# Loads of w by slot, four heads in banks of their own, and the first quarter of w from SyncE as float32

## The chip, the cores and the metric

One core of one Trainium2 chip. The metric is device time in microseconds (us), the median of several runs.

## The reference

```python
B, S, D = (16, 2048, 1024)          # x: B x S x D, w: D x D, decay: D, all float32
xw = x @ w
out[:, 0, :] = xw[:, 0, :]
for t in range(1, S):
    out[:, t, :] = decay * out[:, t - 1, :] + xw[:, t, :]
```

So: a matrix product, then a decayed running sum along S.

## The kernel before

x is cut into 64 chunks of 512 time steps. A chunk is loaded by GpSimd with a cast to bfloat16 (`xb`), turned on VectorE (`xw`), copied to `xt` by ScalarE or VectorE, and multiplied by w on TensorE: two chunks are one group, and each of the 8 column blocks n ("heads") of a group is one tile of 16 matmuls of 512 columns, accumulated in PSUM. A tile is then scanned along time on VectorE. Six of eight tiles are scanned in pairs of steps, for which ScalarE and GpSimd do the other half of the arithmetic; the factor of such a scan is decay squared (`dec2`). The order of all this is a fixed list of deeds per tile, the agenda. w lies in SBUF as `wsb[:, k, ...]` with k = 2m + e: m is a slot of 64 rows in each quarter of 256 rows, e tells even rows from odd ones; q is the quarter of the 128 partitions.

Its parts that change (cut):

```python
dec2 = psp.tile([128, 512], FP32, name="dec2")          # squares of decay, a PSUM bank
...
def load_w(queue, h, e, m0=0, m1=M):                    # 4 loads of 32 partitions
    for q in range(NQ):
        pin(queue.dma_start(
            out=stage[h, e, m0][quad(q)].rearrange("p (m d) -> p m d", m=m1 - m0),
            in_=_ap(w, [[2 * D, P], [2 * P * D, m1 - m0], [1, CH]],
                    (q * CQ + m0 * 2 * P + e) * D + h * CH)))
...
for _ in range(34):                                     # warm-up
    pin(nc.tensor.matmul(out=spare, lhsT=idle[:, 0:128], rhs=idle, start=True, stop=True))
load_w(nc.sync, 0, 0, 0, M // 2)                        # float32; all other loads of w: GpSimd, cast
...
# agenda: M = half a chunk of x, U = a group of loads of w, W/w = copy of w on VectorE/ScalarE,
#         E/F/G = turn and copies of half a chunk, P/S/C/B = a tile's pairing, scan, completion, output
-99: "M0 M1 U0 U1 M2 M3 U2 U3 L L L W0 w1 E0 F0 G0 w3 W2 E1 F1 G1 W4 w5 ...",
...
if step == 0:                                           # three heads with two banks each, one with one
    heads = [ring(psp, "ps", 3, [128, T]) for _ in range(3)]
    firsts = [ps[:, 0:TL] for ps in heads] + [spare]
```

## Time and profile before

| | before |
|---|---|
| time, median of 4 runs beside the changed kernel | 915.33 us (915.03 to 915.55) |
| span of the profiled run | 912.5 us |
| TensorE, VectorE, ScalarE, GpSimd busy | 891, 826, 686, 664 us |
| first real matmul; end of the last | 11.2; 901.6 us |
| half clock of TensorE | only up to 6.6 us, and after its work has ended |

The rest of the reading is in the prediction. Views in order of time show start, duration, line, operation, out<-in, what ended the idle time before. First, VectorE in order of time (start, duration, line, operation, out<-in, what ended the idle time before): the turns of the four half chunks. Three begin as soon as the half chunk has landed; the second landed at 11.2 and waited for another deed.

```profile
8.60 1.25 DVE L115 STREAM_TRANSPOSE xw<-xb 128x1024 f32<-128x1024 f32 x1 [1.55 <-DMA xb<-in_x_dram]
12.87 1.24 DVE L115 STREAM_TRANSPOSE xw<-xb 128x1024 f32<-128x1024 f32 x1
18.61 1.25 DVE L115 STREAM_TRANSPOSE xw<-xb 128x1024 f32<-128x1024 f32 x1 [2.38 <-DMA xb<-in_x_dram]
21.33 1.25 DVE L115 STREAM_TRANSPOSE xw<-xb 128x1024 f32<-128x1024 f32 x1 [0.17 <-DMA xb<-in_x_dram]
```

Second, the time from issue to landing of all twenty loads of w:

```profile
DMA to landing us min/median/max: 2.7/4.4/5.7
```

### The profile page before, as it was taken

Reading aid. Unit: us, or ns where it says so; the run is one execution under the profiler, and the core shown is the slowest. Engines: PE = TensorE matmul, PEld = TensorE weight load, DVE = VectorE, ACT = ScalarE, POOL = GpSimd, SP = SyncE. Lnnn points to the kernel's source line nnn. Section 1 sums busy time; section 2 is a strip of 40 time slices with the busy share of each in tenths; the row PEclk is TensorE's granted clock in tenths of the full one; section 3 lists DMA queues with packets and bytes.
Section 4 is the critical chain, followed back from the end, with each engine's and each line's share of the span. In section 5 each row is a group of like instructions: output and inputs, shape, how many; then the busy total and the mean of one; then the engine's idle time right before and its main releaser. Section 6 shows DMA issues by size and latency. Waiting matters only on the chain.

```text
span 912.5 us, 11926 instructions
## 1 busy us (share of the span) xinstructions
PE 891.3 (98%) x4088; PEld 408.5 (45%) x4170; DVE 826.0 (91%) x613; ACT 685.8 (75%) x950; POOL 664.4 (73%) x764
## 2 busy tenths in 40 slices
PE   8899999999999999999999999999999999999995
PEld 4444444444444444444444444444444444444442
DVE  4999999999999999999999999999999999999986
ACT  3778887877877777778778778778778778777753
POOL 8688878777777777777677777777787776776552
PEclk9999999999999999999999999999999999999998
DMA  9999999999999999999999999999999999999668
GB/s 170 166 220 215 215 230 235 256 250 255 247 237 255 247 237 224 230 233 231 223 235 227 224 231 229 230 226 231 227 224 230 231 230 224 232 229 207 151 151 219
DMA packets 406253, 204.49 MB, mean 224 GB/s; under 512 B 12976, under 2 KB 405936, under 8 KB 406192
## 3 DMA queue, kind: packets, MB, share of 16 engines
q1 hardware_dynamic: 268848, 134.76, 59.5%
q0 software_dynamic: 137344, 68.96, 56.8%
q8 instruction: 32, 0.52, 0.2%
q14 instruction: 29, 0.24, 0.1%
HBM read 138.42 MB, written 134.22 MB: 299 GB/s over the span
## 4 chain that ended last, share of the span: by engine, by line
PE 90%; DMA 3%; POOL 2%; issue 2%; DVE 2%; ACT 1%; SPq 0%; DVEq 0%; POOLq 0%
PE ps L126 90%; DMA xb<-in_x_dram 2%; POOL xb L105 1%; DMA ot<-in_w_dram 1%; DVE so L194 1%; DVE xw L115 1%; POOL ot L245 1%; PE spare L126 0%; DMA out_dram<-ot 0%; DVE so L180 0%; POOL so L208 0%; ACT xt L123 0%; DVE ot L215 0%; POOL xs L174 0%; ACT xs L168 0%
## 5 line engine op out<-in xcount | busy, mean ns | idle before, releaser
L126 PE MATMUL ps<-xt,wsb 128*128 128x512 bf16 (+1 forms) x4011 | 874.2, 377 | 9.0 <-DVE so L194 2.6
L126 PEld LDWEIGHTS <-wsb 128*128 128x128 bf16 x4136 | 404.6, 98 | 485.7 <-issue 5.6
L174 POOL TENSOR_TENSOR xs<-h,xs 128x512 f32<-128x512 f32 (+1 forms) x193 | 245.3, 1271 | 195.5 <-ACT h L158 88.3
L168 ACT COPY xs<-ps 128x1024 f32<-128x1024 f32 (+1 forms) x193 | 191.6, 993 | 158.8 <-PE ps L126 149.3
L215 DVE STREAM_TRANSPOSE ot<-so 128x1024 f32<-128x1024 f32 (+1 forms) x264 | 302.7, 1184 | 1.9 <-POOL so L208 1.1
L208 POOL TENSOR_TENSOR so<-h,xs 128x512 f32<-128x512 f32 (+1 forms) x193 | 244.3, 1266 | 34.5 <-ACT h L158 18.1
L123 ACT COPY xt<-xw 128x2048 bf16<-128x2048 bf16 (+1 forms) x128 | 239.8, 1875 | 7.5 <-DVE xw L115 7.5
L105 POOL DMA_DIRECT2D xb<-in_x_dram x264 | 174.1, 660 | 2.0 <-POOLq L435 0.9
L158 ACT ACTIVATE h<-so,dec 128x512 f32<-128x512 f32 (+1 forms) x193 | 147.1, 763 | 36.0 <-DVE so L180 32.1
L115 DVE STREAM_TRANSPOSE xw<-xb 128x2048 f32<-128x2048 f32 (+1 forms) x66 | 146.7, 2222 | 6.1 <-DMA xb<-in_x_dram 6.1
L180 DVE TENSOR_TENSOR_SCAN so<-dec,keep,xs 128x512 f32<-128x512 f32 (+1 forms) x99 | 121.6, 1229 | 29.8 <-POOL xs L174 29.6
L180 DVE TENSOR_TENSOR_SCAN so<-dec,xs 128x512 f32<-128x512 f32 x94 | 114.8, 1222 | 31.3 <-POOL xs L174 28.2
L158 ACT ACTIVATE h<-ps,dec 128x512 f32<-128x512 f32 (+1 forms) x193 | 131.8, 683 | 0.0
L194 DVE TENSOR_TENSOR_SCAN so<-dec,ps 128x1024 f32<-128x1024 f32 x33 | 74.5, 2261 | 0.0
L194 DVE TENSOR_TENSOR_SCAN so<-dec,keep,ps 128x1024 f32<-128x1024 f32 (+1 forms) x33 | 73.4, 2225 | 0.0
L211 ACT COPY keep<-so 128x1 f32<-128x1 f32 x136 | 25.1, 187 | 0.3 <-DVE so L194 0.3
L173 ACT COPY so<-keep 128x1 f32<-128x1 f32 x99 | 19.0, 192 | 0.7 <-DVE ot L215 0.7
L171 POOL MEMSET so<- 128x1 f32 x94 | 11.0, 117 | 3.2 <-DVE ot L215 3.2
L262 PE MATMUL spare<-idle 128*128 128x512 bf16 x34 | 10.2, 473 | 1.2 <-DVE idle L259 1.2
L126 PE MATMUL spare<-xt,wsb 128*128 128x512 bf16 (+1 forms) x43 | 11.2, 359 | 0.1
L245 POOL DMA_DIRECT2D ot<-in_w_dram x16 | 9.0, 561 | 2.4 <-issue 0.7
L253 ACT COPY wsb<-ot 128x512 bf16<-128x512 bf16 x6 | 3.4, 615 | 5.7 <-DMA ot<-in_w_dram 5.7
(18 smaller groups left out, 20.3 us busy)
## 6 DMA issues: line engine op xcount, KB each, us to landing
out_dram<-ot SPq DMA_DIRECT2D x248, 512.0 KB, 10.6
xb<-in_x_dram POOLq DMA_DIRECT2D x248, 256.0 KB, 7.8
out_dram<-ot SPq DMA_DIRECT2D x12, 256.0 KB, 4.2
xb<-in_x_dram POOLq DMA_DIRECT2D x16, 128.0 KB, 5.0
ot<-in_w_dram POOLq DMA_DIRECT2D x12, 128.0 KB, 5.2
out_dram<-ot SPq DMA_DIRECT2D x8, 128.0 KB, 2.8
ot<-in_w_dram SPq DMA_DIRECT2D x4, 128.0 KB, 3.5
ot<-in_w_dram POOLq DMA_DIRECT2D x4, 64.0 KB, 4.3
```

The costliest lines, as they stand in the source:

```text
L105: pin(nc.gpsimd.dma_start(out=xb_of[c][quad(q), j0:j1], in_=_ap(x, [[D, P], [P * D, j1 - j0], [1, CQ]], (b * S + t0 + j0 * P) * D + q * CQ)))
L115: pin(nc.vector.transpose(out=dst.rearrange("p (m j i) -> p j m i", m=M, i=P)[:, j0:j1], in_=src.rearrange("p (j m c) -> p j m c", m=M, c=P)))
L123: pin(copy(out=xt_of[c][:, m0:m1, :, j0 * P:j1 * P], in_=src))
L126: pin(nc.tensor.matmul(out=ps[:, t0:t1], lhsT=wsb[:, k, n].rearrange("p q i -> p (q i)"), rhs=xt[:, k // 2, k % 2, t0:t1], start=(k == 0 a ...
L158: pin(nc.scalar.activation(out=h, in_=src, func=mybir.ActivationFunctionType.Copy, scale=dec[:, self.n:self.n + 1]))
L168: pin(nc.scalar.copy(out=self.xs, in_=self.ps))
L174: pin(nc.gpsimd.tensor_tensor(out=self.xs[:, 1:T:2], in0=g, in1=self.xs[:, 1:T:2], op=ALU.add))
L180: pin(nc.vector.tensor_tensor_scan(out=so[:, 3:T + 2:2], data0=dec2[:, n:n + 1].to_broadcast([128, T // 2]), data1=self.xs[:, 1:T:2], init ...
L194: pin(nc.vector.tensor_tensor_scan(out=so[:, t:t + size], data0=dec[:, n:n + 1].to_broadcast([128, size]), data1=ps, initial=before, op0=A ...
L208: pin(nc.gpsimd.tensor_tensor(out=so[:, 2:T + 2:2], in0=h, in1=self.xs[:, 0:T:2], op=ALU.add))
L211: pin(nc.scalar.copy(out=self.keep, in_=so[:, T + 1:T + 2]))
L215: pin(nc.vector.transpose(out=self.ot[:, :, n % R * P:(n % R + 1) * P], in_=self.so[:, 2:T + 2].rearrange("p (i t) -> p i t", t=P)))
```

## The change

The intent: w becomes usable slot by slot (one load of 128 partitions brings all that one k needs) instead of only when all four quarters are there; all four heads of the first group run through before the first scan, each with banks of its own; and GpSimd, which issues all the casting loads of both kernels, gives more of w to SyncE. To free a bank for the fourth head the squares of decay move to SBUF, and after some tiles to a spare bank. The core of the diff (cut: bookkeeping for outputs, which keeps the same order; the turns and copies of x in two pieces; the order of the first group's matmuls; and the agenda of steps 0 to 16):

```diff
-    dec2 = psp.tile([128, 512], FP32, name="dec2")
+    squares = [const.tile([128, K], FP32, name="squares")]
 ...
-    def load_w(queue, h, e, m0=0, m1=M):
-        for q in range(NQ):
-            pin(queue.dma_start(
-                out=stage[h, e, m0][quad(q)].rearrange("p (m d) -> p m d", m=m1 - m0),
-                in_=_ap(w, [[2 * D, P], [2 * P * D, m1 - m0], [1, CH]],
-                        (q * CQ + m0 * 2 * P + e) * D + h * CH)))
+    def load_w(queue, i):
+        h, e, m = i // 8, i // 4 % 2, i % 4
+        pin(queue.dma_start(
+            out=stage[h, e][:, m * CH:(m + 1) * CH],
+            in_=_ap(w, [[CQ * D, NQ], [2 * D, P], [1, CH]], (m * 2 * P + e) * D + h * CH)))
 ...
-    for _ in range(34):
+    pin(nc.scalar.copy(out=idle[:, 0:1], in_=idle[:, 1:2]))
+    for _ in range(27):
 ...
-    load_w(nc.sync, 0, 0, 0, M // 2)
+    for m in range(M):
+        load_w(nc.sync, m)
 ...
-        -99: "M0 M1 U0 U1 M2 M3 U2 U3 L L L W0 w1 E0 F0 G0 ...",
+        -99: "M0 M1 U4 U5 U6 U7 M2 M3 U8 U9 U10 U11 U12 U13 w1 U14 L U15 W0 L L L E0 F0 G1 E1 ...",
 ...
-            firsts = [ps[:, 0:TL] for ps in heads] + [spare]
+            firsts = [ps[:, 0:TL] for ps in heads] + [spares[0]]
+            seconds = [ps[:, TL:T] for ps in heads] + [spares[1]]
```

More of the change, by code (lines that the diff above doesn't have):

```diff
@@ L108, in load, with turn @@
                     (b * S + t0 + j0 * P) * D + q * CQ)))
-    def turn(c, j0=0, j1=NJ):
+    def turn(c, j0=0, j1=NJ, m0=0, m1=M):
         if c not in xw_of:
@@ L115, in turn @@
         pin(nc.vector.transpose(
-            out=dst.rearrange("p (m j i) -> p j m i", m=M, i=P)[:, j0:j1],
-            in_=src.rearrange("p (j m c) -> p j m c", m=M, c=P)))
+            out=dst.rearrange("p (m j i) -> p j m i", m=M, i=P)[:, j0:j1, m0:m1],
+            in_=src.rearrange("p (j m c) -> p j m c", m=M, c=P)[:, :, m0:m1]))
     def part(c, copy, m0, m1, j0=0, j1=NJ):
@@ L136, with __init__ @@
     class Tile:
-        def __init__(self, g, n, ps, ot, there):
+        def __init__(self, g, n, ps, outlets):
             self.b, self.t0 = chunks[g[0]]
             self.T = TL * len(g)
-            self.n, self.ps, self.ot, self.there = n, ps, ot, there
-            self.final = g == [nch - 1]
+            self.n, self.ps, self.outlets = n, ps, outlets
             self.paired = n % R != R - 1
@@ L175, in pair, with scan @@
                 out=self.xs[:, 1:T:2], in0=g, in1=self.xs[:, 1:T:2], op=ALU.add))
-        def scan(self):
+        def scan(self, half=None):
             T, n, so = self.T, self.n, self.so
@@ L181, in scan @@
                     out=so[:, 3:T + 2:2],
-                    data0=dec2[:, n:n + 1].to_broadcast([128, T // 2]),
+                    data0=squares[-1][:, n:n + 1].to_broadcast([128, T // 2]),
                     data1=self.xs[:, 1:T:2],
@@ L193, in scan @@
                     t = 2 + i * size
-                    pin(nc.vector.tensor_tensor_scan(
-                        out=so[:, t:t + size],
-                        data0=dec[:, n:n + 1].to_broadcast([128, size]),
-                        data1=ps,
-                        initial=before,
-                        op0=ALU.mult,
-                        op1=ALU.add,
-                    ))
+                    if half in (None, i):
+                        pin(nc.vector.tensor_tensor_scan(
+                            out=so[:, t:t + size],
+                            data0=dec[:, n:n + 1].to_broadcast([128, size]),
+                            data1=ps,
+                            initial=before,
+                            op0=ALU.mult,
+                            op1=ALU.add,
+                        ))
                     before = so[:, t + size - 1:t + size]
@@ L211, in complete, with back, __init__, store @@
                 pin(nc.scalar.copy(out=self.keep, in_=so[:, T + 1:T + 2]))
-        def back(self):
-            T, n = self.T, self.n
-            pin(nc.vector.transpose(
-                out=self.ot[:, :, n % R * P:(n % R + 1) * P],
-                in_=self.so[:, 2:T + 2].rearrange("p (i t) -> p i t", t=P)))
-            self.there.add(n)
-            size = 2 if self.final and n >= R else R
-            n0 = n // size * size
-            if self.there.issuperset(range(n0, n0 + size)):
-                self.store(n0, n0 + size)
-        def store(self, n0, n1):
-            c0 = n0 % R * P
-            size = (n1 - n0) * P
-            for q in (0, 2, 1, 3):
-                pin(nc.sync.dma_start(
-                    out=_ap(out, [[D, P], [P * D, self.T // P], [1, size]],
-                            (self.b * S + self.t0) * D + n0 // R * CH + q * CR + c0),
+        def back(self, half=None):
+            n, c0 = self.n, self.n % R * P
+            for outlet in self.outlets:
+                if half not in (None, outlet.half):
+                    continue
+                t0, nj = outlet.t0, outlet.nj
+                pin(nc.vector.transpose(
+                    out=outlet.ot[:, :, c0:c0 + P],
+                    in_=self.so[:, 2 + t0:2 + t0 + nj * P].rearrange(
+                        "p (i t) -> p i t", t=P)))
+                outlet.missing.remove(n)
+                if not outlet.missing:
+                    outlet.store(self.b, self.t0)
+    class Outlet:
+        def __init__(self, ns, nj, half=0, queues=(nc.sync,)):
+            self.ns, self.missing, self.half = ns, set(ns), half
+            self.nj, self.t0, self.queues = nj, half * nj * P, queues
+            self.ot = ot_tile(nj)
+        def store(self, b, t0):
+            n0 = self.ns[0]
+            c0 = n0 % R * P
+            size = len(self.ns) * P
+            for i, q in enumerate((0, 2, 1, 3)):
+                pin(self.queues[i % len(self.queues)].dma_start(
+                    out=_ap(out, [[D, P], [P * D, self.nj], [1, size]],
+                            (b * S + t0 + self.t0) * D + n0 // R * CH + q * CR + c0),
                     in_=self.ot[quad(q), :, c0:c0 + size]))
@@ L236 @@
     size = M * CH
-    stage = {(0, 0, 0): room[0][:, 0:size // 2],
-             (0, 0, M // 2): room[0][:, size // 2:size * 3 // 4].bitcast(BF16),
-             (0, 1, 0): room[0][:, size:size * 3 // 2].bitcast(BF16),
-             (1, 0, 0): room[1][:, 0:size // 2].bitcast(BF16),
-             (1, 1, 0): room[1][:, size // 2:size].bitcast(BF16)}
-    def load_w(queue, h, e, m0=0, m1=M):
-        for q in range(NQ):
-            pin(queue.dma_start(
-                out=stage[h, e, m0][quad(q)].rearrange("p (m d) -> p m d", m=m1 - m0),
-                in_=_ap(w, [[2 * D, P], [2 * P * D, m1 - m0], [1, CH]],
-                        (q * CQ + m0 * 2 * P + e) * D + h * CH)))
+    stage = {(0, 0): room[0][:, 0:size],
+             (0, 1): room[0][:, size:size * 3 // 2].bitcast(BF16),
+             (1, 0): room[1][:, 0:size // 2].bitcast(BF16),
+             (1, 1): room[1][:, size // 2:size].bitcast(BF16)}
+    def load_w(queue, i):
[3 more added lines that the diff above has]
+            in_=_ap(w, [[CQ * D, NQ], [2 * D, P], [1, CH]], (m * 2 * P + e) * D + h * CH)))
     def settle(h, e, m, copy):
-        m0 = M // 2 if (h, e) == (0, 0) and m >= M // 2 else 0
-        src = stage[h, e, m0][:, (m - m0) * CH:(m - m0 + 1) * CH]
+        src = stage[h, e][:, m * CH:(m + 1) * CH]
         pin(copy(out=wcols[:, 2 * m + e, h],
@@ L274, in load_half, with part_one @@
             load(i // 2, q, *halves[i % 2])
-    def load_part(i):
-        load_w(nc.gpsimd, *((0, 0, M // 2, M), (0, 1), (1, 0), (1, 1))[i])
+    def part_one(i, copy):
+        part(i // 8, copy, i % 4, i % 4 + 1, *halves[i // 4 % 2])
     def settle_one(i, copy):
@@ L285, in decays, with square, square_again @@
             out=dec.rearrange("p (h r) -> p h r", h=2), in_=cols[:, :, 0:R]))
-        pin(nc.vector.tensor_tensor(out=dec2[:, 0:K], in0=dec, in1=dec, op=ALU.mult))
+        square(0)
+    def square(i):
+        pin(nc.vector.tensor_tensor(
+            out=squares[-1][:, 0:K], in0=dec, in1=dec, op=ALU.mult))
+    def square_again(i):
+        squares.append(ring(psp, "spare1", 1, [128, TL]))
+        square(0)
     slots = [(g, n) for g in groups[:-1] for n in range(K)]
@@ L311 @@
         "M": load_half,
-        "U": load_part,
-        "E": lambda i: turn(i // 2, *halves[i % 2]),
-        "F": lambda i: part(i // 2, nc.vector.tensor_copy, 0, 2, *halves[i % 2]),
-        "G": lambda i: part(i // 2, nc.scalar.copy, 2, M, *halves[i % 2]),
-        "f": lambda i: part(i // 2, nc.vector.tensor_copy, 2, M, *halves[i % 2]),
-        "D": decays,
+        "U": lambda i: load_w(nc.gpsimd, i),
+        "E": lambda i: turn(i // 4, *halves[i // 2 % 2], i % 2 * 2, i % 2 * 2 + 2),
+        "F": lambda i: part_one(i, nc.vector.tensor_copy),
+        "G": lambda i: part_one(i, nc.scalar.copy),
+        "D": decays,
+        "d": square_again,
+        "Z": lambda s: tiles[s % len(slots)].scan(1),
+        "z": lambda s: tiles[s % len(slots)].scan(0),
+        "b": lambda s: tiles[s % len(slots)].back(1),
+        "a": lambda s: tiles[s % len(slots)].back(0),
         "L": lambda i: load(*loads.pop(0)) if loads else None,
@@ L320 @@
     agenda = {
-        -99: "M0 M1 U0 U1 M2 M3 U2 U3 L L L W0 w1 E0 F0 G0 w3 W2 E1 F1 G1 W4 w5 W6 w7 E2 F2 D G2 E3 F3 G3 W8 W9 W10 W11",
-        0: "w12 L L w13 P0 S0",
-        1: "w14 L P1 L",
-        2: "S1 W15 P2 B0 S2",
-        3: "T2 L S3 C0 C1 C2",
-        4: "L P4 X2 L Y2 L B2 T3 B1 L",
-        5: "P5 C3 X3 L S4",
-        6: "B3 L Y3 S5 L P6 C5 C4 T4",
-        7: "S7 S6 X4 L C7 C6 B5 B4 B7",
-        8: "",
-        9: "P8 B6 S8 P9 L L T5 C8",
-        10: "P10 L L S9 L C9 L B8",
-        11: "X5 S10 L C10 S11 B9",
-        12: "P12 L B11 B10 C11 Y4",
-        13: "P13 S12 T6 Y5 C12 L",
-        14: "S13 P14 C13 L B12 L L",
-        15: "S15 X6 S14 C14 B13",
-        16: "L P16 B14 B15 Y6 L L",
+        -99: "M0 M1 U4 U5 U6 U7 M2 M3 U8 U9 U10 U11 U12 U13 w1 U14 L U15 W0 L L L E0 F0 G1 E1 L F2 G3 E2 F4 G5 W2 E3 F6 w3 G7 w5 W6 w7 W4 E4 F8 G9 E5 F10 G11 E6 G13 W8 F12 E7 F14 L G15 D W9 W10 W11",
+        0: "L P0",
+        1: "w13 w14 S0",
+        2: "L P1 P2 S1 L S2 w12 B0",
+        3: "L C0 w15 C1 C2 T2",
+        4: "P4 S3 X2 B2 B1 L T3 Y2",
+        5: "S4 C3 L",
+        6: "L P5 L B3 L L T4 P6 X3 Y3 S5 C4",
+        7: "S7 L C5 X4 S6 C6 B7 d B5",
+        8: "B4 L B6 P8 C7",
+        9: "P9 S8",
+        10: "L T5 S9 C8 P10",
+        11: "L X5 S11 L L L C9 Y4 S10 C10",
+        12: "B8",
+        13: "B11 B9 P12 B10 S12 L Y5 L P13 C12",
+        14: "P14 T6 Y6 L S13 C13",
+        15: "L S15 S14 C14 L",
+        16: "B13 P16 B12 B15 X6 B14 C11 L",
         -16: "P-16 B-17 S-16 C-16 C-17",
@@ L356 @@
     flips = (0, 1, -2, -15, -8)
+    halved = ()
     later = {10: ["Y4"]}
@@ L382 @@
     perform(agenda[-99].split())
+    spares = [spare] + [ring(psp, "spare1", 1, [128, TL])]
     for step, (g, n) in enumerate(slots):
         T = TL * len(g)
+        left = step - len(slots)
         if n % R == 0:
-            ot, there = ot_tile(NJ * len(g)), set()
+            ns, nj = range(n, n + R), T // P
+            outlets = [Outlet(ns, nj)]
+        if left in (-R, 2 - R):
+            outlets = [Outlet(range(n, n + 2), nj)]
+        if left in halved and left - 1 not in halved:
+            ns = range(n, K)
+            outlets = [Outlet(ns, nj // 2, 0), Outlet(ns, nj // 2, 1, (nc.sync, nc.scalar))]
@@ L387 @@
         if step == 0:
             heads = [ring(psp, "ps", 3, [128, T]) for _ in range(3)]
-            firsts = [ps[:, 0:TL] for ps in heads] + [spare]
+            firsts = [ps[:, 0:TL] for ps in heads] + [spares[0]]
+            seconds = [ps[:, TL:T] for ps in heads] + [spares[1]]
             for j0, j1 in halves:
-                for k in range(0, K, 2):
+                for k in (0, 2):
                     for i in range(R):
                         matmul(firsts[i], i, k, xt_of[0], j0 * P, j1 * P)
-            for k in range(1, K, 2):
+            for k in (4, 6, 1, 3, 5, 7):
@@ L395 @@
                 for i in range(R):
                     matmul(firsts[i], i, k, xt_of[0])
-            for j0, j1 in halves:
-                for i in range(3):
-                    for k in range(K):
-                        matmul(heads[i][:, TL:T], i, k, xt_of[1], j0 * P, j1 * P, j0 * P)
-        if step < R:
-            if n < 3:
-                ps, second = heads[n], heads[n][:, TL:T]
-            else:
-                second = ring(psp, "ps", 3, [128, TL])
-                ps = (spare, second)
-            if n >= 3:
+            for k0 in range(0, K, 4):
+                for i in range(R):
+                    for k in range(k0, k0 + 4):
+                        matmul(seconds[i], i, k, xt_of[1], 0, H * P)
@@ L408 @@
+            for i in range(R):
+                for k in range(K):
+                    matmul(seconds[i], i, k, xt_of[1], H * P, TL, H * P)
+        if step < R:
+            ps = heads[n] if n < 3 else tuple(spares)
+        elif left in halved:
+            ps = tuple(ring(psp, "ps", 3, [128, TL // 2]) if n < K - 1 or i == 0
+                       else ring(psp, "spare", 1, [128, TL // 2]) for i in range(2))
+            for i in range(2):
                 for k in range(K):
-                    matmul(second, n, k, xt_of[1])
+                    pin(nc.tensor.matmul(
+                        out=ps[i], lhsT=wsb[:, k, n].rearrange("p q i -> p (q i)"),
+                        rhs=xt_of[g[0]][:, k // 2, k % 2, i * TL // 2:(i + 1) * TL // 2],
+                        start=(k == 0), stop=(k == K - 1)))
@@ L414 @@
                 ps = ring(psp, "spare", 1, [128, TL])
-            for k in range(K):
-                for l, c in enumerate(g):
-                    matmul(ps[:, l * TL:(l + 1) * TL], n, k, xt_of[c])
-        tiles.append(Tile(g, n, ps, ot, there))
-        left = step - len(slots)
+            todo = [(k, l) for k in range(K) for l in range(len(g))]
+            if step == K:
+                todo.sort(key=lambda kl: kl[1])
+            for k, l in todo:
+                matmul(ps[:, l * TL:(l + 1) * TL], n, k, xt_of[g[l]])
+        tiles.append(Tile(g, n, ps, outlets))
         do = agenda.get(step, agenda.get(left) if left >= -2 * K else None)
```

## The prediction

Step 14 from 65.7 to 64.1, 1.6 us and a few tenths more if small bubbles go, so 915.26 - 1.7 = about 913.5.

> **What bounds the kernel now.** I read the page first (engine shares), then who waited for whom on TensorE, then TensorE in order of time, then the chain of waits for the first 70 us.
>
> ```profile
> span 912.5 us, 11926 instructions
> PE 891.3 (98%) x4088; PEld 408.5 (45%) x4170; DVE 826.0 (91%) x613; ACT 685.8 (75%) x950; POOL 664.4 (73%) x764
> ```
>
> TensorE is busy almost the whole span, so what matters is where it is not doing real work. The real work is 64 chunks x 8 tiles x 8 slices of w = 4096 matmuls of 512 columns. In the chain of waits one unbroken group of them runs from 83.84 to 94.63, 10.79 us; if that is 50 matmuls (49 recorded, one missing) the pitch is 0.2158 us, and 4096 x 0.2158 = 884 us. Real matmuls start at 11.20 and end at 901.6 (the last group starts at 899.69 and takes 1.89). So 912.5 = 11.2 ahead of them + 884 + about 6.4 of bubbles + 10.9 of tail. Only the 11.2 and the 6.4 can be changed by this diff; the tail's agenda is not touched.
>
> ```profile
> PE ps L126 <- DVE so L194: 2.6, 4, 1.2
> PE ps L126 <- DVE xt L123: 1.2, 2, 0.8
> PE ps L126 <- DVE wsb L253: 0.8, 1, 0.8
> ```
>
> These three rows (waiter, releaser, total, times, longest) are 4.6 of the 6.4 us; the rest is refilling the pipeline after each gap (a recorded 128x512 matmul lasts 0.38 against a pitch of 0.22) and a slack stretch of half-width matmuls. Where they lie, TensorE in order of time:
>
> ```profile
> 20.64 5.70 PE L126 MATMUL ps<-xt,wsb 128*128 128x256 bf16 x48 [0.39 <-DVE xt L123]
> 27.59 1.89 PE L126 MATMUL ps<-xt,wsb 128*128 128x512 bf16 x7 [1.25 <-DVE so L194]
> 29.77 7.07 PE L126 MATMUL ps<-xt,wsb 128*128 128x512 bf16 x32 [0.29 <-DVE so L194]
> 37.69 27.79 PE L126 MATMUL ps<-xt,wsb 128*128 128x512 bf16 x125 [0.86 <-DVE so L194]
> 65.71 54.55 PE L126 MATMUL ps<-xt,wsb 128*128 128x512 bf16 x247 [0.23 <-DVE so L194]
> ```
>
> After 65.71 TensorE never stops until the last chunks: whatever time step 14 (the one that starts at 65.71) is moved by is what the whole kernel is moved by. The group at 37.69 begins with step 6 of the agenda (a step is one tile, 16 matmuls, 3.453 us), so step 8 starts at 44.6 and step 10 at about 51.5 (37.69 + 4 x 3.453). Every one of the four waits on L194 is for a scan on VectorE that reads its tile straight from PSUM and has to free the slot.
>
> Two more things feed this. First, transfers: the chain of waits runs
>
> ```profile
> 12.02 4.67 POOL xb L105 x8
> 16.69 5.38 DMA ot<-in_w_dram
> 22.08 0.28 issue
> 22.36 2.02 POOL xb L105 x3
> 24.38 8.03 DMA xb<-in_x_dram
> ```
>
> and the landings recorded in the trace come one behind the other: the first half of chunk 0 complete at 8.5, the second at 11.2, w's parts at 12.5 and 15.6, chunk 1's halves at 18.5 and 21.2, the second half of w at 24.1 and 27.1, chunk 2 at 32.4. A load of 32 x 2048 elements of x (256 KB read) lands every 0.66 us, about 390 GB/s read; this stream has no hole. Second, VectorE, by stage:
>
> ```profile
> core 0: us, PE busy (x) PEld busy (x) DVE busy (x) ACT busy (x) POOL busy (x), PEclk, DMA share, GB/s
> 28.00:36.00 8.00, 7.69 (x35) 3.42 (x35) 7.33 (x6) 5.51 (x11) 4.06 (x6) 1.00 1.45 196
> 36.00:44.00 8.00, 7.09 (x33) 3.15 (x33) 7.89 (x7) 7.50 (x7) 4.81 (x7) 1.00 1.15 142
> 44.00:50.00 6.00, 6.00 (x30) 2.69 (x29) 6.00 (x5) 5.73 (x9) 5.21 (x7) 1.00 0.95 130
> ```
>
> From 36 to 50 us VectorE is full (13.89 of 14). A TensorE that is let loose earlier meets a VectorE with nothing to spare.
>
> [...] Here warm-up matmuls go at 0.427 us until 6.5 us and then at 0.216; [...] the slow time was 5.3 us.
>
> **The change, part by part.**
> Loads. SyncE now sends 1 MB of w instead of 0.5 MB before the first scans; GpSimd sends four transfers by slot instead of eight. Total bytes up to chunk 1 are the same (2 MB of w, 4 MB of x), so at one rate chunk 1 still lands at 21.2, w by 27, chunk 2 at 32.4. But 0.5 MB of w now comes ahead of x: 0.5 MB / 390 GB/s = 1.3 us, so chunk 0's first half moves from 8.5 to about 9.7 and its second from 11.2 to about 12.5.
> Start. Turns and copies are cut in two: before, 1.25 (turn) + 0.69 (copy) to the first operand; now about 0.69 (a 128x512 transpose at the tail) + 0.30 (a 128x512 bf16 copy), 0.95 less. The warm-up, 27 instead of 34 but held back for ScalarE's table load (1.28 us), ends at 10.1 to 10.6. First real matmul: 9.7 + 0.1 + 0.69 + 0.30 + 0.1 = about 10.9, against 11.20. Then a hole until chunk 0's second half (about 13.6), then 12 us of work mostly gapless: k = 4 at 15.2, the rest of chunk 0 to 20.4, chunk 1's first half for four heads to 23.85, its second half to 27.35.
> Banks. n = 3's second chunk is now inside that run (8 matmuls, 1.73 us), where before it waited 1.25 us for a scan. Step 4 can begin when the first scan ends, about 27.6; but its k = 1 needs a copy of w that ScalarE does after it has emptied head 2 (done on TensorE 26.45, copy 1.0, scaled copy 0.7, w 0.6: 28.8). Step 4 thus really runs to 31.9, steps 5 to 7 follow at 31.9, 35.3, 38.8. Before, step 6 started at 37.69: 2.4 us gained here, and the ring slot that waited for n = 3's scan (0.86 us) is gone.
> What is given back. VectorE's first scan starts at 24.9 to 25.3, as before (25.26), and the turn of chunk 2 still waits for its landing at 32.4 (before, 32.87). From there to the end of S7 the same eleven instructions stand in the list (before: 32.87 to 49.82, 16.95 us), so S7 again ends at about 49.8, and step 10 needs its slot. Also chunk 3's turn now comes after one output transpose more (39.9 to 42.1 instead of 38.70 to 40.97), its two copies on ScalarE (1.9 each) end at 46.0, and step 8, ready at 42.3, must wait for the second: it ends at 46.85 instead of 45.75. Step 10 then starts at 50.3 against 51.5. From S7's end to S11's the new order needs 13 us against 15.9, so step 14 is not held: 50.3 + 13.8 = 64.1 against 65.71.
> Sum: 65.7 - 64.1 = 1.6 us, and a few tenths more if the small bubbles go. 915.26 - 1.7 = about 913.5.
>
> **Rivals.** (1) Full gain: VectorE and ScalarE keep up, step 6's 2.4 us and the 0.2 us wait at 65.71 both arrive at the end, and the stall for w at step 4 is smaller: 3 us, 912.2. For it: the new agenda looks tuned to the new times. Against: VectorE 13.89 of 14 busy. (2) Nothing gained: the float32 next to the casting loads holds x back by more than 1.3 us, or a later turn of chunk 3 costs more; step 14 stays at 65.7, 915.3. For it: everything early is bound by bytes, and the bytes are the same. (3) The clock falls back: from 12 to 15 us TensorE works less than half the time; if half clock returned for some microseconds, first scans come 3 us later, and step 14 1 to 2 us later: 916.5. Against: before had holes of 0.8 us there without it.
>
> **Range and chances.** The three terms (bytes, VectorE's chain, ScalarE's copies) each have about 1 us of doubt, and the gain cannot exceed the 6.4 us of bubbles plus about 1 us of start; nothing comes near 2% (18 us). 913.5, range 911.4 to 915.3; within 2% is all but certain.
>
> **What would show it.** Right: chunk 0's first half lands near 9.7, chunk 1 near 21 and chunk 2 near 32.4; no wait for L194 (now for the same scan's line) between 27 and 40; S7 ends near 49.8; step 14 starts near 64.1; after it TensorE is unbroken and the tail is 10.9 us. Wrong: landings later than these by over 1 us, half clock after 10 us, or step 10 starting below 49 (then VectorE was not the limit I took it for).

## The result, and the profile after

| | before | after |
|---|---|---|
| time, median of 4 | 915.33 us | 926.40 us (926.17 to 927.67) |
| ratio, fast runs of the same rounds | | 1.0127 (1.0111 to 1.0143) |
| first real matmul | 11.2 us | 15.9 us |
| end of the last matmul | 901.6 us | 913.8 us |
| tail after it | 10.9 us | 10.6 us |

A ratio is the mean time of one kernel's fast runs over that of the other's of the same rounds, so not quite the ratio of the medians. The changed kernel is 11.1 us (1.3%) slower; within 2%, but far outside the predicted range of 911.4 to 915.3. The page's head, and who TensorE waited for:

```profile
span 924.4 us, 11912 instructions
PE 893.1 (97%) x4081; PEld 408.6 (44%) x4163; DVE 828.3 (90%) x621; ACT 687.2 (74%) x956; POOL 663.9 (72%) x760
```

```profile
PE ps L126 <- DVE xt L123: 9.8, 3, 4.9
PE ps L126 <- ACT wsb L262: 4.0, 1, 4.0
PE ps L126 <- DVE so L194: 0.4, 1, 0.4
```

Busy times are as before; TensorE simply stood still longer. The waits for scans (L194) have nearly gone, as intended, but 13.8 us of waits for x and w have come. TensorE in order of time:

```profile
15.86 0.80 PE L126 MATMUL ps<-xt,wsb 128*128 128x256 bf16 x3 [4.93 <-DVE xt L123]
...
22.08 0.80 PE L126 MATMUL ps<-xt,wsb 128*128 128x256 bf16 x3 [4.36 <-DVE xt L123]
...
42.06 98.17 PE L126 MATMUL ps<-xt,wsb 128*128 128x512 bf16 x438 [3.95 <-ACT wsb L262]
```

The turns on VectorE, to set against those of before (each half chunk is now turned in two pieces; these are the first pieces; the view puts the first wait down to a load of w, but what landed just before, at 14.5, is the half chunk itself):

```profile
14.63 0.71 DVE L115 STREAM_TRANSPOSE xw<-xb 128x512 f32<-128x512 f32 x1 [8.37 <-DMA ot<-in_w_dram]
...
20.85 0.71 DVE L115 STREAM_TRANSPOSE xw<-xb 128x512 f32<-128x512 f32 x1 [3.97 <-DMA xb<-in_x_dram]
...
26.62 0.71 DVE L115 STREAM_TRANSPOSE xw<-xb 128x512 f32<-128x512 f32 x1 [2.42 <-DMA xb<-in_x_dram]
...
30.26 0.71 DVE L115 STREAM_TRANSPOSE xw<-xb 128x512 f32<-128x512 f32 x1 [1.31 <-DMA xb<-in_x_dram]
```

The four half chunks came at 14.6, 20.9, 26.6 and 30.3 us instead of 8.6, 11.2 (its turn waited until 12.9 for another deed), 18.6 and 21.3. And the loads of w:

```profile
DMA to landing us min/median/max: 6.6/8.2/15.2
```

This view leaves out a load that shows fewer than 16 increments (see below), so in after it counts only GpSimd's twelve. The page gives those twelve, the same bytes in both kernels, by themselves; first of before, then of after:

```profile
ot<-in_w_dram POOLq DMA_DIRECT2D x12, 128.0 KB, 5.2
```

```profile
ot<-in_w_dram POOLq DMA_DIRECT2D x12, 128.0 KB, 8.2
```

They took 1.6 times as long at the median. The trace also holds every increment of every DMA semaphore, and they point to why. In before each SyncE load of w shows 16 increments, as many as the page counts DMA engines, all within 0.6 to 1.7 us. In after each of SyncE's four shows one jump at once and then only four increments: the first load at 5.39 to 5.78, the second at 10.8 to 11.4, the third at 14.9 to 15.4, the fourth at 19.0 to 19.5. I read this as four engines carrying these loads, one load after the other. The trace does not name the engine of a packet, but its DMA packets agree: from 6 us to 19.5, when the last of these loads is in, SyncE's queue never has more than 4 packets under way at once, where in before it has up to 19 (at 2.4 us). The last GpSimd load of chunk 0's first half had 12 of its 16 increments by 8.54, when all of before's were in (8.48); its last four came at 14.15 to 14.51. GpSimd's own issuing then fell behind too: it sat idle for 6.7 us in all until loads of x had landed before it could issue loads of w, and issued chunk 1's loads from 16.8 to 25.2 us instead of 12.0 to 16.1.

What differs in SyncE's loads by slot, besides their size (256 KB for 128), is the pattern: by slot, the source begins with a dimension of 4 (the quarters), and each load shows four increments after its jump; by quarters it begins with 32, and each shows 16. So the reading, theory A below, is that the outermost dimension of the source sets how many engines carry a load on this queue. SyncE's 1 MB then lies on four engines, while each load of x shows 16 increments and its half chunk is turned only after the last of them (14.51, turn at 14.63). On GpSimd's queue the number does not tell: its loads by slot show 16 increments too, but spread out (the first one in after has 12 by 12.4 us and the last four at 22.8 to 23.2). That the four lag because they are the same four engines for all is a reading; the experiments test what the source pattern does.

### The profile page after: what moved, and what is told of

Its sections match the earlier page's. It is cut to its first block, busy times and chain, and to the rows that moved or that the text cites. A ratio compares the mean times of both kernels' runs of the same rounds, so it can differ in the third digit from the quotient of the medians.

```text
span 924.4 us, 11912 instructions
## 1 busy us (share of the span) xinstructions
PE 893.1 (97%) x4081; PEld 408.6 (44%) x4163; DVE 828.3 (90%) x621; ACT 687.2 (74%) x956; POOL 663.9 (72%) x760
## 4 chain that ended last, share of the span: by engine, by line
PE 93%; DMA 3%; issue 1%; POOL 1%; DVE 1%; ACT 0%; DVEq 0%; POOLq 0%
PE ps L126 93%; DMA ot<-in_w_dram 3%; DMA xb<-in_x_dram 1%; POOL ot L256 0%; PE spare L126 0%; DVE ot L219 0%; DVE so L194 0%; POOL xb L105 0%; POOL xs L173 0%; ACT xs L167 0%; ACT wsb L262 0%; ACT h L157 0%; DVEq L485 0%; DVEq L219 0%; ACT so L172 0%
## 5 line engine op out<-in xcount | busy, mean ns | idle before, releaser
L105 POOL DMA_DIRECT2D xb<-in_x_dram x264 | 174.0, 660 | 10.6 <-DMA ot<-in_w_dram 4.8
L157 ACT ACTIVATE h<-so,dec 128x512 f32<-128x512 f32 (+1 forms) x193 | 147.3, 763 | 31.7 <-DVE so L179 28.2
L115 DVE STREAM_TRANSPOSE xw<-xb 128x2048 f32<-128x2048 f32 (+1 forms) x70 | 147.3, 2104 | 16.1 <-DMA ot<-in_w_dram 8.4
L179 DVE TENSOR_TENSOR_SCAN so<-spare,keep,xs 128x512 f32<-128x512 f32 (+1 forms) x99 | 121.6, 1229 | 30.5 <-POOL xs L173 30.3
L179 DVE TENSOR_TENSOR_SCAN so<-spare,xs 128x512 f32<-128x512 f32 x90 | 110.1, 1223 | 30.8 <-POOL xs L173 27.7
L194 DVE TENSOR_TENSOR_SCAN so<-dec,ps 128x1024 f32<-128x1024 f32 x33 | 74.5, 2261 | 0.0
L194 DVE TENSOR_TENSOR_SCAN so<-dec,keep,ps 128x1024 f32<-128x1024 f32 (+1 forms) x33 | 73.4, 2225 | 0.0
L211 ACT COPY keep<-so 128x1 f32<-128x1 f32 x136 | 25.2, 186 | 0.0
L126 PE MATMUL spare<-xt,wsb 128*128 128x512 bf16 (+1 forms) x58 | 13.8, 353 | 0.1
L170 POOL MEMSET so<- 128x1 f32 x94 | 10.9, 116 | 1.0 <-DVE ot L219 1.0
L179 DVE TENSOR_TENSOR_SCAN so<-squares,xs 128x512 f32<-128x512 f32 x4 | 5.7, 1428 | 3.5 <-POOL xs L173 3.5
```

Source lines behind the costliest of these rows:

```text
L105: pin(nc.gpsimd.dma_start(out=xb_of[c][quad(q), j0:j1], in_=_ap(x, [[D, P], [P * D, j1 - j0], [1, CQ]], (b * S + t0 + j0 * P) * D + q * CQ)))
L115: pin(nc.vector.transpose(out=dst.rearrange("p (m j i) -> p j m i", m=M, i=P)[:, j0:j1, m0:m1], in_=src.rearrange("p (j m c) -> p j m c", ...
L126: pin(nc.tensor.matmul(out=ps[:, t0:t1], lhsT=wsb[:, k, n].rearrange("p q i -> p (q i)"), rhs=xt[:, k // 2, k % 2, t0:t1], start=(k == 0 a ...
L157: pin(nc.scalar.activation(out=h, in_=src, func=mybir.ActivationFunctionType.Copy, scale=dec[:, self.n:self.n + 1]))
L179: pin(nc.vector.tensor_tensor_scan(out=so[:, 3:T + 2:2], data0=squares[-1][:, n:n + 1].to_broadcast([128, T // 2]), data1=self.xs[:, 1:T:2 ...
L194: pin(nc.vector.tensor_tensor_scan(out=so[:, t:t + size], data0=dec[:, n:n + 1].to_broadcast([128, size]), data1=ps, initial=before, op0=A ...
```

## The experiments

Theory A: few engines per load. Rival B: float32 on SyncE beside casting loads lowers the rate. Rival C: TensorE's half clock after an idle start makes most of it. Rival D: the banks and the agenda cost something themselves. Later, theory E: squares in SBUF make VectorE wait. Before was run in the same rounds each time, and the ratio is to it.

| run | time, us | before beside it | ratio (95%) |
|---|---|---|---|
| e1_rows (wrong) | 916.45 | 915.36 | 1.0000 (0.9977 to 1.0022) |
| e2_quarters | 916.05 | 915.36 | 1.0001 (0.9984 to 1.0018) |
| e3_sp_quarters | 919.07 | 915.36 | 1.0035 (1.0018 to 1.0052) |
| e4_pool_quarters | 924.73 | 915.36 | 1.0099 (1.0077 to 1.0121) |
| e5_old_loads | 915.55 | 916.06 | 0.9998 (0.9986 to 1.0011) |
| e6_old_loads_agenda | 915.75 | 916.06 | 1.0005 (0.9992 to 1.0017) |
| e7_before_sp_full | 915.18 | 916.06 | 0.9997 (0.9983 to 1.0010) |
| e8_quarters_warm | 915.69 | 916.06 | 1.0003 (0.9990 to 1.0015) |
| e9_squares_early | 914.75 | 915.18 | 0.9994 (0.9982 to 1.0007) |
| e11_tuned | 913.22 | 915.18 | 0.9979 (0.9967 to 0.9992) |
| e10_before_sbuf_squares | 918.57 | 915.18 | 1.0040 (1.0026 to 1.0054) |
| e12_before_slots | 921.06 | 915.18 | 1.0063 (1.0047 to 1.0078) |

When the last load of each part was complete (us, from the sixteenth increments in the traces), for the kernels that change loads:

| | before | after | e1 | e2 | e3 | e4 | e5 | e7 |
|---|---|---|---|---|---|---|---|---|
| chunk 0, first half | 8.5 | 14.5 | 10.9 | 11.0 | 11.5 | 15.6 | 8.5 | 11.2 |
| chunk 0, second half | 11.2 | 20.7 | 13.7 | 13.7 | 14.2 | 21.6 | 11.2 | 13.9 |
| chunk 1, second half | 21.2 | 30.1 | 21.7 | 21.7 | 24.4 | 30.1 | 21.9 | 21.9 |
| second half of w | 27.1 | 41.3 | 31.2 | 28.9 | 34.4 | 36.7 | 27.7 | 27.8 |
| chunk 2 | 32.4 | 45.3 | 35.0 | 32.8 | 38.5 | 41.2 | 33.1 | 33.2 |

**e1_rows.** Same destinations, bytes, queues and number of loads; only the source's outermost dimension is 128 instead of 4. The rows of w end up in wrong places, so the result is wrong.

```diff
-            in_=_ap(w, [[CQ * D, NQ], [2 * D, P], [1, CH]], (m * 2 * P + e) * D + h * CH)))
+            in_=_ap(w, [[2 * D, 128], [1, CH]], (m * CQ + e) * D + h * CH)))
```

> Wrong result on purpose: each by-slot load of w reads 128 rows in one even step instead of four blocks of 32 rows; bytes, number of loads, destinations, queues, float32 on SyncE and all waits stay. Theory A (a load whose source begins with a dimension of 4 is carried by 4 of the 16 DMA engines): the four SyncE loads of w land within 2 us of each other by about 6.5 us instead of 5.8, 11.4, 15.4 and 19.5; chunk 0's first half is there at about 9.7 instead of 14.5, chunk 1 at about 21 instead of 29.6, and the time is about 913.5 (911.5 to 915.5). Rival B (float32 on SyncE beside casting loads on GpSimd is what halves the rate): nothing changes, 924 to 927. Rival C (half clock of TensorE after an idle start makes most of it): also about as after, since only the loads change.

It fell to 916.45 us, the ratio to before from 1.0127 to 1.0000. SyncE's loads now show 16 increments each and were complete at 3.4, 4.6, 6.7 and 9.1, not all by 6.5 as expected, chunk 0 came 1.2 us later than expected, and the time is 0.95 us above the range given for A. B foresaw 924 and more and falls as the main cause. C is not separated by this run: the half clock went with the loads, from 13.7 us of it in after to 3.4 here (more under e8_quarters_warm). A stands.

**e2_quarters.** The mapping that is right, with a source that begins with 32 and so, by theory A, with all 16 engines: 4 loads of 32 partitions for each group of four slots.

```diff
-        h, e, m = i // 8, i // 4 % 2, i % 4
+        h, e, q = i // 8, i // 4 % 2, i % 4
         pin(queue.dma_start(
-            out=stage[h, e][:, m * CH:(m + 1) * CH],
-            in_=_ap(w, [[CQ * D, NQ], [2 * D, P], [1, CH]], (m * 2 * P + e) * D + h * CH)))
+            out=stage[h, e][quad(q)].rearrange("p (m d) -> p m d", m=M),
+            in_=_ap(w, [[2 * D, P], [2 * P * D, M], [1, CH]], (q * CQ + e) * D + h * CH)))
```

> Right result: the same bytes of w in as many loads, but each load is one quarter of the partitions (32) with all four slots, so its outermost dimension is 32. Theory A: all 16 engines carry it, time about 914 (912 to 916); a little worse than the wrong-rows run, since a slot is usable only when all four loads of its group have landed. Rival B: float32 is still on SyncE beside the casting loads, so 922 to 927.

916.05 us, 0.05 above the range. Issue to landing of w in this run:

```profile
DMA to landing us min/median/max: 3.8/5.1/7.0
```

Here the view counts all sixteen loads; by the page, GpSimd's twelve alone have a median of 5.1, against 5.2 in before, with SyncE's float32 still there. So the whole loss of 11 us is in how the loads of w were cut.

**e3_sp_quarters and e4_pool_quarters.** The same edit for SyncE's four loads alone, and for GpSimd's twelve alone.

```diff
+        if queue is nc.sync:          # e4: nc.gpsimd
+            (by quarters, as in e2_quarters)
+        else:
+            (by slot, as in the change)
```

> Only SyncE's four loads by quarters; GpSimd's twelve stay by slot. Theory A: chunk 0 as in the run with all by quarters (first half near 9.7), chunk 1 near 21 to 23, but the second half of w and chunk 2 still some 4 us late as in after, so 917 to 921. Rival B: 924 to 927.

> Only GpSimd's twelve loads by quarters; SyncE's four stay by slot. Theory A: SyncE's loads still land at about 5.8, 11.4, 15 and 19 and chunk 0 still at 14.5 and 20.7; only what GpSimd's slots cost after chunk 1 comes back, about 4 us: 920 to 924. If the two parts' gains (this run and the run with SyncE alone by quarters) add up to the gain of the run with both, within 2 us, each load's cost is its own; if not, one hides the other.

Measured: 919.07, so GpSimd's slots cost 3.0 us over e2_quarters (0.34% by the ratios), and 924.73, so SyncE's slots cost 8.7 us (0.98%). Together 11.7, against 10.4 for both at once (926.40, of other rounds, less 916.05): nearly additive, within the 2 us that was set. In e4 SyncE's loads completed at 6.8, 12.4, 16.3 and 20.4, the same staircase as in after (1.0 to 1.4 us later than stated).

**e12_before_slots.** The same cause alone, in the kernel before: three of its GpSimd groups of w by slot.

```diff
+        if m1 - m0 == M:
+            for m in range(M):
+                pin(queue.dma_start(
+                    out=stage[h, e, 0][:, m * CH:(m + 1) * CH],
+                    in_=_ap(w, [[CQ * D, NQ], [2 * D, P], [1, CH]], (m * 2 * P + e) * D + h * CH)))
+            return
```

> The kernel before with three of its four GpSimd groups of w loaded by slot (twelve loads of the same bytes, source beginning with a dimension of 4); nothing else. Theory A says that this alone costs what GpSimd's slots cost in the change: 2 to 5 us, 917.5 to 920.5, with increments of one load's semaphore split into a group that arrives early and one that comes microseconds later. If the harm needs SyncE's loads as well: within 0.7 us of before.

921.06 us, ratio 1.0063: the harm is confirmed without anything else of the change, and is half a microsecond over the range given. Chunk 1 was complete at 25.0 instead of 21.2, and the clock fell to half twice (15.4 to 18.8 and 32.4 to 35.8 us), which belongs to this number.

**e7_before_sp_full.** The other half of the loads' change alone, in before: SyncE sends the whole first quarter as float32, by quarters; GpSimd four loads fewer (cut: the staging buffer).

```diff
-    load_w(nc.sync, 0, 0, 0, M // 2)
+    load_w(nc.sync, 0, 0)
-        -99: "M0 M1 U0 U1 M2 ...
+        -99: "M0 M1 U1 M2 ...
```

> The kernel before, with only SyncE's part changed: it sends the whole first quarter of w as float32, by quarters of the partitions, and GpSimd four loads fewer. Rival B (float32 beside casting loads is the harm): 922 or more. Theory A with the estimate of the prediction (0.5 MB more ahead of x): chunk 0's halves land 1.3 to 2.5 us later than 8.5 and 11.2, chunk 1 within 0.7 us of 21.2, and the time is 0 to 1.5 us over before: 915.3 to 917.

No difference to before (0.9997). Chunk 0 comes 2.7 us later, about twice the prediction's 1.3, and the first real matmul starts at 13.30 instead of 11.20; but chunk 1 is 0.7 us late only, and the end shows none of it within the interval. B is out: float32 beside casting loads delayed what stands behind it (chunk 0 by 2.7 us) and cost nothing at the end (0.9997). The later start of TensorE cost nothing here.

**e8_quarters_warm.** e2_quarters with 34 warm-up matmuls instead of 27.

```diff
-    for _ in range(27):
+    for _ in range(34):
```

> The run with all loads by quarters, and 34 warm-up matmuls instead of 27, so that TensorE is busy until chunk 0 arrives at about 12.2 us. Theory C (the half clock from about 15 to 17.5 us is from the hole after the warm-up): full clock throughout, chunk 0 done on TensorE 1.5 us earlier; at the end 0 to 1.5 us less than 916.05, less if the copies of w and VectorE set the pace after that.

915.69 against 916.05, no difference beyond the intervals, and not the test it was meant to be: the half clock was still there, at 15.9 to 19.3 instead of 14.5 to 17.9, and the next hole (1.70 us, before chunk 0's second half) remained too. In after the clock was half from 14.5 to 24.7 and from 41.8 to 45.2. The second of these lies on the path: 8 matmuls at 0.43 instead of 0.216 us, some 1.7 us. The half clock goes with the loads: e2 to e4, which differ in loads only, have 3.4, 6.8 and 13.7 us of it. How much of the 8.7 and 3.0 us it makes is not told apart, but theory C cannot be most of the loss: TensorE was busy for 4.5 and 3.1 us in after's two stretches of half clock, so they cost at most half of that, an estimate of 3.8 of the 11.1 us.

**e5_old_loads.** With the loads out of the way, what do the four heads, the cut turns and the new agenda do? The changed kernel with before's `load_w` and before's order of loads (cut: `load_w` itself).

```diff
-    for m in range(M):
-        load_w(nc.sync, m)
+    load_w(nc.sync, 0, 0, 0, M // 2)
-        -99: "M0 M1 U4 U5 U6 U7 M2 M3 U8 U9 U10 U11 U12 U13 w1 U14 L U15 W0 L L L E0 ...
+        -99: "M0 M1 U0 U1 M2 M3 U2 U3 L w1 W0 L L L E0 ...
```

> The changed kernel with the loads of w as before the change (SyncE half of the first quarter as float32, the rest from GpSimd by quarters of the partitions); four heads in banks of their own, cut turns and copies and the new agenda stay. If the loads alone are to blame (theory A with the larger float32 part), chunk 0's halves land at 8.5 and 11.2 and chunk 1 at 21.2 as before, the clock stays at full, and the time is at or under that of before: 912 to 915. If the banks and the agenda themselves cost something (rival D), it stays near the run with all by quarters, 915.5 to 917.

Full clock from 7.4 us on, loads as in before, and yet 0.9998: the gain of 1.7 us of the prediction is not there, nor any net cost. That does not clear D: 915.55 lies 0.55 above A's range and inside D's, though before itself had 916.06 here, and a gain and a cost can cancel. Counted from the trace at 16 matmuls a step, step 6 starts at about 37.5, where before has 37.69 and the prediction 35.3: the start came no earlier. VectorE, in order of time, shows what held it (read from the trace; in e6, which moves that copy, the scan starts at 25.83). The new agenda was made for loads by slot; with quarters, a copy of w that stands ahead of chunk 1's copies waits for its loads, TensorE waits 1.35 and 0.48 us for those copies, and the first scan starts at 27.54 instead of 25.26:

```profile
24.61 0.29 DVE L265 COPY wsb<-ot 128x512 bf16<-128x512 bf16 x1 [1.90 <-DMA ot<-in_w_dram]
...
27.54 4.45 DVE L194 TENSOR_TENSOR_SCAN so<-dec,ps 128x1024 f32<-128x1024 f32 x2
```

A second, smaller delay comes later:

```profile
51.02 2.01 DVE L179 TENSOR_TENSOR_SCAN so<-squares,xs 128x512 f32<-128x512 f32 x1
...
54.10 1.14 DVE L302 TENSOR_TENSOR spare<-dec 128x8 f32<-128x8 f32 x1
```

A scan that takes 1.2 us took 2.01, and squaring 8 numbers per partition took 1.14 where it took 0.17 in before. GpSimd was in an addition just then, from 50.64 for 1.30 us: 50.64 + 1.30 = 51.94, and the scan ended 1.09 later, as if it had begun only then. The squaring ended at 55.24, and GpSimd's next addition (from 53.91 for 1.29 us) at 55.20. The reading, theory E: a VectorE instruction whose two inputs are both in SBUF can be held up while GpSimd adds there, though not each time (the four such scans took 1.18 to 2.01 us). Before, `dec2` in PSUM kept the scans to one SBUF input.

**e10_before_sbuf_squares.** That cost by itself, in before, for all paired scans.

```diff
-    dec2 = psp.tile([128, 512], FP32, name="dec2")
+    dec2 = const.tile([128, K], FP32, name="dec2")
```

> The kernel before with its squares of decay in SBUF instead of a PSUM bank, for all 193 paired scans. Theory E: many scans then wait for GpSimd's additions (1.27 us each) or make them wait; the mean scan grows from 1.22 us to between 1.4 and 1.7, VectorE's busy time from 826 to 860 to 910, and the kernel gets slower by 0.5 to 5 per cent. If the place of the squares does not matter: same scan, same time.

The groups of instructions by shape, first of before, then of this run:

```profile
L180 DVE TENSOR_TENSOR_SCAN so<-dec,xs 128x512 f32<-128x512 f32 x94 | 114.8, 1222 | 31.3 <-POOL xs L174 28.2
```

```profile
L180 DVE TENSOR_TENSOR_SCAN so<-dec,xs 128x512 f32<-128x512 f32 x94 | 154.6, 1645 | 2.7 <-POOL xs L174 2.7
```

The mean scan grows from 1222 to 1645 ns and VectorE's busy time from 826 to 889 us, as E expected; the time by 0.40%, just under the range. The longer "busy" mostly replaces idle time that was there (28.2 us of waiting for GpSimd's addition has become 2.7). The profiled execution is the slowest of the four (920.81), and its clock was at half from 70.8 to 74.3 us, after TensorE had waited 2.75 us for a scan; what that adds to the 0.40% is not told apart.

**e9_squares_early.** e5_old_loads, with the squaring into the spare bank (`d`) right after the scan that empties it.

```diff
-        4: "P4 S3 X2 B2 B1 L T3 Y2",
+        4: "P4 S3 d X2 B2 B1 L T3 Y2",
-        7: "S7 L C5 X4 S6 C6 B7 d B5",
+        7: "S7 L C5 X4 S6 C6 B7 B5",
```

> As e5_old_loads, but the squares of decay go to the spare PSUM bank right after the scan that empties it, four scans earlier. In the change four scans read the squares from SBUF while GpSimd reads SBUF too: one of them took 2.01 us instead of 1.2 and the squaring itself 1.14 instead of 0.17. Theory E (these two inputs from SBUF make VectorE wait for GpSimd, and VectorE sets the pace here): the scan is back at 1.2, TensorE's two waits of 0.37 and 0.35 us at 55.5 and 59.4 us shrink or go, and the time falls by 0.4 to 1.2 us. If VectorE does not set the pace: under 0.3 us.

In the trace the effect is exactly there:

```profile
39.57 0.18 DVE L302 TENSOR_TENSOR spare<-dec 128x8 f32<-128x8 f32 x1
...
51.85 1.20 DVE L179 TENSOR_TENSOR_SCAN so<-spare,xs 128x512 f32<-128x512 f32 x1
```

and both waits of TensorE for ScalarE (0.37 and 0.35 us) are gone, while a new one of 0.33 us, for a copy of chunk 3, stands at 48.0. In time it is 0.9994, at the low end of what was expected and not to be told from none by the interval.

**e6_old_loads_agenda.** e5_old_loads, with the copies of w's second half moved.

```diff
-        -99: "... G13 W8 F12 E7 F14 L G15 D W9 W10 W11",
-        0: "L P0",
-        2: "L P1 P2 S1 L S2 w12 B0",
+        -99: "... G13 F12 E7 F14 L G15 D W8 W9 W10 W11",
+        0: "L w12 P0",
+        2: "L P1 P2 S1 L S2 B0",
```

> As e5_old_loads, but two deeds of the agenda moved to suit loads by quarters: ScalarE's copy of w for k = 1 of the second half comes ahead of the other two and of emptying head 2, and VectorE's copy for k = 0 after chunk 1's last turn. In the run with all by quarters TensorE waited 2.1 us for that copy; if that wait is on the path, 1 to 2 us less than e5_old_loads; if VectorE's chain behind it sets the pace, within 0.5 us of it.

A miss: 1.0005. TensorE does start step 4 at 28.15 instead of 29.87, but the copies now stand ahead of emptying head 2 on ScalarE, VectorE waits 2.39 us for it, and TensorE gets its time back as two waits for ScalarE's copies of chunk 3:

```profile
46.16 1.02 PE L126 MATMUL ps<-xt,wsb 128*128 128x512 bf16 x4 [1.54 <-ACT xt L123]
47.95 47.73 PE L126 MATMUL ps<-xt,wsb 128*128 128x512 bf16 x212 [0.78 <-ACT xt L123]
```

In this execution, the slowest of the five (917.05), the clock then also fell to half, from 48.0 to 51.4 us; whether it did in the others is not known.

**e11_tuned.** Before's loads, squares early, and an agenda that keeps VectorE's chain first: head 2 is emptied before the copies of w; chunk 3 is turned one output transpose earlier, as in before; its first copy comes before head 6 is emptied.

```diff
 (to e6_old_loads_agenda)
-        0: "L w12 P0",
-        1: "w13 w14 S0",
-        2: "L P1 P2 S1 L S2 B0",
+        0: "L P0",
+        1: "S0",
+        2: "L P1 P2 w12 w13 w14 S1 L S2 B0",
-        4: "P4 S3 X2 B2 B1 L T3 Y2",
+        4: "P4 S3 d X2 B2 L T3 B1 Y2",
-        6: "L P5 L B3 L L T4 P6 X3 Y3 S5 C4",
-        7: "S7 L C5 X4 S6 C6 B7 d B5",
+        6: "L P5 X3 L B3 L L T4 P6 Y3 S5 C4",
+        7: "S7 L C5 X4 S6 C6 B7 B5",
```

> An attempt at a version better than both: e9_squares_early with the agenda of the first sixteen steps put right for loads by quarters (head 2 emptied before w's second half is copied, chunk 3 turned before one output transpose, its first copy before head 6 is emptied). If the early gain of four heads can be carried to the end: 912.5 to 914.5 against 915.3 to 916.0 of before on the same chip. If VectorE's chain takes it back whatever the order: as before within 0.5 us.

913.22 us, ratio 0.9979 (0.9967 to 0.9992): faster than before by about 2 us and than the change by 13, with a right result.

```profile
28.96 16.14 PE L126 MATMUL ps<-xt,wsb 128*128 128x512 bf16 x74 [0.25 <-ACT wsb L265]
...
47.06 53.26 PE L126 MATMUL ps<-xt,wsb 128*128 128x512 bf16 x246 [1.95 <-ACT xt L123]
```

After this group TensorE waits once more, 1.95 us at 47.06 for a copy of chunk 3, and then not again in the start. By the same count step 6 starts at about 35.4 and step 8 at 42.3, both 2.3 us earlier than in before, and step 14 at 65.2, only 0.5 us earlier: most of the early gain is given back at that copy. Against before's trace (of another chip, and of an execution 1.1 us under the median) the span is 1.3 us shorter: 0.5 at TensorE's end, and 0.7 in a tail of 10.2 instead of 10.9 us, for which no run gives a reason. So a part of the early gain can be carried to the end, where VectorE and ScalarE are given the order for it. Which of the four edits does how much was not told apart.

## Why the prediction was wrong, point by point

- **"Total bytes up to chunk 1 are the same, so at one rate chunk 1 still lands at 21.2."** This is the step that failed. Chunk 1 landed at 30.1. I took 390 GB/s as a property of the bytes, while I had measured it on loads that each showed 16 increments close together; by slot each of SyncE's loads of w showed four. I had seen the new source pattern begin with 4, and drew nothing from it. Undoing it alone (e2_quarters) brings 926.40 to 916.05. My reading that the landings keep to one rate on either queue was thin: all landings after 6.5 us in before are of GpSimd's loads. Two of the prediction's own signs of being wrong came: landings over 1 us late, and half clock after 10 us.
- **"0.5 MB of w ahead of x: 1.3 us."** Right in kind, too small: with 16 increments for each of SyncE's loads chunk 0 came 2.5 us later (8.5 to 11.0 in e2_quarters, 2.7 in e7), and it did not matter at the end (e7: 0.9997).
- **"Then a hole, then mostly gapless; the clock falls back" as rival 3.** It did fall back, in the changed kernel and still for 3.4 us in e2_quarters. I argued against it from before's holes of 0.8 us; in e2_quarters it happened with two holes of 1.40 and 1.68 us, 1.0 us of work between them; in e7, with holes of 1.75 and 0.80 us, it did not, so no threshold follows. (The slow time of before's warm-up was 5.4 us, from 1.20 to 6.61, not 5.3.)
- **Rival 2 named the right place and the wrong reason**: x held back by float32 on SyncE. e1_rows and e2_quarters keep that float32 and are not slow.
- **The banks' gain, 1.6 us.** The waits for L194 between 27 and 40 us did go (0.4 us left). Without the loads' harm the gain was zero in e5_old_loads, which is no fair test, since its agenda did not fit its loads. My account of VectorE's chain also missed a term: four scans with two SBUF inputs and the squaring, 0.8 + 1.0 us in that trace, because the PSUM bank of the squares was the one given to the fourth head; taking it out alone (e9) changed the ratio by 0.0004, within the intervals. With a matching agenda (e11_tuned) the early steps are where the prediction had them (step 6 at 35.4 for 35.3, step 8 at 42.3), but chunk 3's copy then costs 1.95 us where 1.1 was predicted, and step 14 starts at 65.2 for 64.1. That the time still falls by about the predicted size (0.9979, about 1.9 us) is in part luck: other loads, another agenda and a shorter tail are in it.
- **What held:** the tail is unchanged (10.6 against 10.9 us), TensorE is unbroken from 42.1 us on, and so the whole kernel moves by what its start moves by.

## What to carry to other kernels

Before recutting a load, look at the outermost dimension of its source. Here SyncE's loads of w showed four increments with 4 and 16 with 32 or 128 (after, e2_quarters, e1_rows), which is read as the number of DMA engines that carry a load, and the four-increment loads also held up GpSimd's loads of x under way with them (chunk 0's first half came at 14.5 instead of 8.5 us). A trace told it at once: on SyncE's queue in the number of increments per load, on GpSimd's in a group that arrives early while a few come late (12 by 8.54 us, the last four at 14.15 to 14.51). And when a buffer moves from PSUM to SBUF to free a bank, count the SBUF inputs of whoever reads it, above all on VectorE next to a busy GpSimd: in e10_before_sbuf_squares the mean scan went from 1222 to 1645 ns.
